# Hybrid SSD and attention step: four z tiles moved into the scan's code, the rest of the projection dealt out two query blocks later

## The chip, the cores and the metric

One core of one Trainium2 chip runs the whole program. The metric is device microseconds of one execution; lower is better. The kernel before takes 1961.51 us (median of 3 runs, 1960.96 to 1962.06).

## What is computed

One step of two trunk layers for 512 prompt tokens and 8 sample tokens (520 columns in all), width 1024. Layer 0 mixes a Mamba-2 scan and a sparse attention with one input and one output projection; layer 1 is a convolution module; a gated feed-forward network follows each. The change touches layer 0 alone:

```python
def ab_project(xn, pos, w_in):
    proj = xn @ w_in
    z, xbc, dt_raw, q, kvc, kvs, kvw, gates = jnp.split(proj, ...)
...
def mamba_branch(z, xbc, dt_raw, ...):
    xbc = jax.nn.silu(causal_dwconv(xh, conv_w, conv_b))
    xs, bm, cm = jnp.split(xbc, ...)
    ...
    y, h_T = ssd_scan(xs, dt, a, bm, cm, h0, SSM_CHUNK)
    y = y.astype(xs.dtype) + d_skip[:, None] * xs
    y = y.reshape(bsz, t, D_INNER) * jax.nn.silu(z)
    y = rms_norm(...)
...
def mixer_ab(xn, ...):
    y_ssm, new_hist, h_T = mamba_branch(...)
    y_nsa = nsa_fn(q, gates, kvc, kvs, kvw)
    out = jnp.concatenate([y_ssm, y_nsa], axis=-1) @ w_out
```

## The kernel before

Everything stands transposed, features on partitions and the 520 tokens in two halves of 256 and 264 columns. Float32 products are made of three products of split operands (`mm3`, L311 to L313: high by high, high by low, low by high), so one 128-row tile of a projection is 8 x 3 x 2 = 48 matmuls.

The mixer of layer 0 has these stages. The queries, keys and values are projected and the sample's cache is compressed (to 270 us). Then come 40 **xz tiles** (`xz_tile`, L992): ten for each of the scan's four groups g, of which t = 0 to 3 are x, 4 and 5 are B and C (these six run through a causal convolution on VectorE), and t = 6 to 9 are z. Each tile is silu'd through a scratch tile (`u_`, `uc`, `uth`) and spilled to DRAM. The first 10 (XZ0) are written ahead of the attention, the others inside it: 16 **query blocks** (4 head groups of 4 blocks; block b of a group attends to b + 1 key blocks, so the fourth is the largest), and after block `step` the code issues the tiles that the table XZF gives it (L1213):

```python
for n in range(*(XZ0 + int((40 - XZ0) * XZF[i]) for i in (step, step + 1))):
    xz_tile(n // 10, n % 10)
```

Next is the **scan** (`scan_group`, L1300): 4 groups of 4 row tiles t, which read the spilled x, z, B and C back. Beside the scan runs the output projection: `nsa_out` (L1286) loads the attention's result (8 `ynl` tiles), splits each into a high and a low part (`x0hn`, `x0ln`, `x1hn`, `x1ln`), and returns `part`, which makes one of 8 output tiles of 48 matmuls (`wo`). It is called once ahead of the first group, and `beside(t)` calls `part` as the table PARTS says. Groups 0 and 1 are then normalised (`gated`), split, and projected beside groups 2 and 3.

The order of the work on each engine is not that of the code: the program is built with a list scheduler that pulls an instruction forward where its operands, buffers and engine are free by its own timeline. It can carry a tile across the blocks and stages around it. The `zt` buffers (3, tag "zt") are shared by the z tiles of the scan and by `ynl`; the split input of the projection (`x0hm`, `x1hm` and their low parts) and that of the output projection (`x0hn` and so on) share one buffer each, so no `ynl` can be split before the last xz tile's products are done.

Of the kernel before, what the change touches and what calls it, by code (L numbers as in the profile page):

```python
# [11 lines left out]
F32 = mybir.dt.float32  # L12
# [13 lines left out]
T = S + NB  # L26
# [8 lines left out]
XZ0 = 10  # L35
# [24 lines left out]
SKEW = (3, 2)  # L60
SQN = 4
PARTS = (0, 0, 0, 3, 0, 0, 2, 2, 0, 0, 0, 3, 0, 0, 2, 2)
XZF = tuple(n / 16 for n in range(17))
VTB = 2
BES = (2, 1)
NST = 16
# [191 lines left out]
def step_kernel(ctx: ExitStack, tc: tile.TileContext, I, O):  # L258
# [423 lines left out]
    def mixer(begin):  # L682
# [25 lines left out]
        ux = ExitStack()  # L708
        up = ux.enter_context(tc.tile_pool(name="mu", bufs=1, side="right"))
        uth = up.tile([128, T], F32, name="uth")  # L710
        ax = ExitStack()
        ap = ax.enter_context(tc.tile_pool(name="ma", bufs=1))

# [4 lines left out]
        vnew = ap.tile([64, 128], F32, name="vnew")  # L718
        pnT = ap.tile([64, 128], F32, name="pnT")
        pti = ap.tile([1, 64], I32, name="pti")  # L720
        u_ = ap.tile([128, T], F32, name="u")
        uc = ap.tile([128, T], F32, name="uc")
        hp = ap.tile([128, 24, NB], F32, name="shp")
        stg = ap.tile([128, 24, 11], F32, name="sstg")
# [7 lines left out]
        for hf in range(2):  # L732
            x.append(tp.tile([128, KD, 266], F32, tag="big", bufs=BIG, name="x"))
            n = HALF[hf][1] - X0[hf]
# [227 lines left out]
        for op in ORDER.split():  # L962
            n = int(op[1:])
# [26 lines left out]
        turns = []  # L990
# [109 lines left out]
        def attention(hg, rows_of):  # L1100
# [3 lines left out]
            for b in range(4):  # L1104
# [105 lines left out]
                        sample(step)  # L1210
                for _ in range(HCN[step]):
                    next(rows_of, None)
                for n in range(*(XZ0 + int((40 - XZ0) * XZF[i]) for i in (step, step + 1))):  # L1213
                    xz_tile(n // 10, n % 10)

        def group_loads(g, q=nc.sync):
# [38 lines left out]
            pass  # L1255
        group, rows = group_loads(0, nc.gpsimd), row_loads(0, 0, nc.gpsimd)
        sample_end()
        nc.sync.dma_start(O["o_sc"], stg.rearrange("p a b -> p (a b)"))
        bp.close()
        ax.close()  # L1260
# [157 lines left out]

        sn4 = tp.tile([128, 16], F32, name="sn4")
        nc.vector.tensor_scalar_mul(sn4, VV("sn"), 0.25)  # L1420
        part = nsa_out()
        todo = iter(range(8))
        for kg in range(2):
            for g in (2 * kg, 2 * kg + 1):

                def beside(t):
                    for m in itertools.islice(todo, PARTS[4 * g + t]):
                        part(m)
                scan_group(g, beside)
            for g in (2 * kg, 2 * kg + 1):  # L1430
                gated(g)
            for m in todo:
                part(m)
            yx = {hf: new_x("s", hf) for hf in range(2)}
            for g in (2 * kg, 2 * kg + 1):
                parted(g, yx)
            if kg == 0:
                todo = iter(range(8))

                def part(m, yx=yx):  # L1440
                    w = wout(0, m)
                    for hf in range(2):
                        out_block(0, yx, m, hf, w, False)
# [252 lines left out]
```

## Time and profile before

| what | before |
|---|---|
| median of 3 runs | 1961.51 us |
| profiled execution, its own time | 1961.93 us |
| its span in the trace | 1959.4 us |
| TensorE (PE) busy | 93% of the span |
| VectorE (DVE) busy | 73% |
| ScalarE (ACT) busy | 50% |
| attention, blocks 0 to 15 | 272 to 667 us |
| last product of an xz tile | 609 us |
| scan, from its first product of states to the last group's | 672 to 836 us |

A matmul's duration in a row is its latency: the next one starts long before it ends. What a matmul costs the engine is read from the distance between two starts. The granted clock (PEclk) is a share of full speed: 1.00 is 2.4 GHz, 0.50 is 1.2 GHz, and a number between is a stretch with both.

### The profile page before, as it was taken

The page shows a single profiled execution, that of the slowest core. Times are in us where ns is not written, and L with a number is a line of the kernel's source. Part 1 is how long each engine was busy: PE and PEld are TensorE (multiplying, and loading weights), DVE is VectorE, ACT ScalarE, POOL GpSimd, SP SyncE. Part 2 cuts the span into 40 slices and gives each one's busy share as a digit, 9 for nine tenths or more (in the row PEclk, how much of TensorE's full clock was granted, in tenths as well). Part 3 has the DMA queues.
Part 4 walks back from the last instruction along what each step waited for, and adds up shares of the span by engine and source line. Part 5 has one row for each costly group of instructions (what it writes and reads, how often), then busy time and mean ns, then how long its engine had stood idle before and what let it go on. Part 6 is the DMA issues. An engine that isn't in the chain of part 4 may idle for free.

```text
span 1959.4 us, 37959 instructions
## 1 busy us (share of the span) xinstructions
PE 1822.2 (93%) x14411; PEld 1702.3 (87%) x14411; DVE 1424.0 (73%) x3404; ACT 971.4 (50%) x2091; POOL 184.1 (9%) x226
## 2 busy tenths in 40 slices
PE   6998899999998799998999999997998899999997
PEld 5997888988887588988999999987867889999997
DVE  5764768888887698968667766575776865666766
ACT  3223546676666577656555433354126755444433
POOL 0000021111000013130000211000100000000000
PEclk9999998999998799999999999998998999999999
DMA  8446254444421274543245433221443223333411
GB/s 289 120 139 191 77 195 130 144 145 123 132 90 55 87 244 138 162 137 106 86 139 170 132 105 109 87 80 52 103 138 104 87 86 113 122 122 120 149 62 49
DMA packets 125946, 240.89 MB, mean 123 GB/s; under 512 B 16499, under 2 KB 63236, under 8 KB 125444
## 3 DMA queue, kind: packets, MB, share of 16 engines
q1 hardware_dynamic: 120676, 221.45, 36.6%
q0 software_dynamic: 4000, 13.73, 2.3%
q10 hardware_dynamic: 1088, 3.29, 0.5%
q8 instruction: 113, 1.85, 0.4%
q14 instruction: 69, 0.57, 0.1%
HBM read 200.75 MB, written 30.88 MB: 118 GB/s over the span
## 4 chain that ended last, share of the span: by engine, by line
PE 41%; DVE 6%; ACT 3%; DMA 2%; SPq 2%; issue 2%; POOL 0%; DVEq 0%; ACTq 0%; POOLq 0%
PE up L311 8%; PE up L312 8%; PE up L313 8%; PE dn L311 4%; PE dn L312 4%; PE dn L313 4%; SPq L607 2%; PE pw L311 1%; PE pw L312 1%; PE pw L313 1%; PE dn L622 1%; DVE sq L328 1%; DVE facc L629 1%; DVE xf L384 1%; DVE h L386 1%
## 5 line engine op out<-in xcount | busy, mean ns | idle before, releaser
L311 PE MATMUL dn<-gh,wh_dn 128*128 128x256 f32 (+1 forms) x704 | 197.4, 285 | 3.3 <-ACT gh L462 2.6
L313 PE MATMUL dn<-gh,wl_dn 128*128 128x256 f32 (+1 forms) x704 | 198.6, 283 | 0.0
L312 PE MATMUL dn<-gl,wh_dn 128*128 128x256 f32 (+1 forms) x704 | 198.2, 283 | 0.0
L450 DVE SCALAR_TENSOR_TENSOR c<-up,vec,c 128x511 f32<-128x511 f32 (+2 forms) x216 | 139.0, 646 | 15.0 <-ACT c L447 14.6
L311 PEld LDWEIGHTS dn<-gh,wh_dn 128*128 128x128 f32 x704 | 131.5, 188 | 4.7 <-ACT gh L462 2.9
L312 PEld LDWEIGHTS dn<-gl,wh_dn 128*128 128x128 f32 x704 | 132.9, 189 | 0.2
L313 PEld LDWEIGHTS dn<-gh,wl_dn 128*128 128x128 f32 x704 | 132.5, 188 | 0.0
L463 POOL TENSOR_TENSOR gl<-gm,gh 128x520 fp32r<-128x520 f32 (+2 forms) x54 | 61.8, 1144 | 702.4 <-ACT gh L462 702.3
L445 DVE TENSOR_TENSOR up<-up,rsx 128x520 f32<-128x520 f32 (+2 forms) x108 | 65.0, 604 | 82.9 <-PE up L313 81.0
L477 DVE TENSOR_TENSOR facc<-dn,facc 128x256 f32<-128x256 f32 (+1 forms) x160 | 66.3, 424 | 66.6 <-PE dn L313 66.3
L292 ACT ACTIVATE wh_up<-raw_up 128x1024 fp32r<-128x1024 f32 x68 | 72.0, 1058 | 70.2 <-PE up L312 47.0
L311 PE MATMUL acc<-x0hm,wh_xz 128*128 128x256 f32 x320 | 96.8, 302 | 5.8 <-ACT u L999 3.4
L293 DVE TENSOR_TENSOR wl_up<-raw_up,wh_up 128x1024 fp32r<-128x1024 f32 x68 | 83.1, 1222 | 20.8 <-ACT wh_up L292 20.4
L313 PE MATMUL acc<-x0hm,wl_xz 128*128 128x256 f32 x320 | 95.0, 297 | 0.0
L312 PE MATMUL acc<-x0lm,wh_xz 128*128 128x256 f32 x320 | 94.7, 296 | 0.0
L447 ACT ACTIVATE c<-up,vec 128x520 f32<-128x520 f32 (+2 forms) x108 | 74.8, 695 | 36.3 <-DVE up L445 35.7
L312 PE MATMUL acc<-x1lm,wh_xz 128*128 128x264 f32 x320 | 92.7, 290 | 0.0
L311 PE MATMUL acc<-x1hm,wh_xz 128*128 128x264 f32 x320 | 92.6, 289 | 0.0
L313 PE MATMUL acc<-x1hm,wl_xz 128*128 128x264 f32 x320 | 92.2, 288 | 0.0
L292 ACT ACTIVATE wh_dn<-raw_dn 128x1024 fp32r<-128x1024 f32 (+1 forms) x48 | 47.4, 988 | 89.0 <-PE dn L312 63.6
L293 DVE TENSOR_TENSOR ptl<-pT,pth 128x512 fp32r<-128x512 f32 (+1 forms) x96 | 65.0, 684 | 25.4 <-ACT pth L292 25.1
L292 ACT ACTIVATE pth<-pT 128x512 fp32r<-128x512 f32 (+1 forms) x96 | 56.2, 595 | 51.5 <-PE pT L1184 49.5
(584 smaller groups left out, 6851.1 us busy)
## 6 DMA issues: line engine op xcount, KB each, us to landing
raw_up<-in_w_up SPq DMA_DIRECT2D x68, 512.0 KB, 3.7
raw_xz<-in_w_in SPq DMA_DIRECT2D x40, 512.0 KB, 4.8
raw_dn<-in_w_down SPq DMA_DIRECT2D x32, 512.0 KB, 3.6
raw_wo<-in_w_out SPq DMA_DIRECT2D x24, 512.0 KB, 4.4
raw_pw<-in_w_pw SPq DMA_DIRECT2D x24, 512.0 KB, 3.6
spill<-uth SPq DMA_DIRECT2D x40, 260.0 KB, 2.0
st<-in_st SPq DMA_DIRECT2D x40, 256.0 KB, 3.9
cc<-in_c_cmp SPq DMA_DIRECT2D x64, 128.0 KB, 2.6
```

The source lines that it names most:

```text
L292: nc.scalar.activation(hi, src, AF.Copy)
L293: (eng or nc.vector).tensor_sub(lo, src, hi.bitcast(F32))
L311: nc.tensor.matmul(ps, hi[:, wc], xh, start=first, stop=False)
L312: nc.tensor.matmul(ps, hi[:, wc], xl, start=False, stop=False)
L313: nc.tensor.matmul(ps, lo[:, wc], xh, start=False, stop=last)
L328: nc.vector.tensor_add(acc[:, :n], acc[:, :n], sq[:, :n])
L445: nc.vector.tensor_mul(u(a, e0), u(a, e0), rv[:, a:e0])
L447: nc.scalar.activation(c[:, rs], u(r0, r1), AF.Identity, bias=V("fb", l * 44 + mt), scale=W(2, mt))
L450: nc.vector.scalar_tensor_tensor(c[:, a:e], u(a - d, e - d), W(2 - d, mt), c[:, a:e], op0=ALU.mult, op1=ALU.add)
L463: nc.gpsimd.tensor_sub(gl[:, rs], gm[:, rs], gh[:, rs].bitcast(F32))
L477: nc.vector.tensor_add(f, ps, f)
L607: nc.sync.dma_start(x4[m][j * 32:j * 32 + 32, i, a:b], glu[m][i * 32:i * 32 + 32, 1 + j + a:1 + j + b])
```

## The change

Three things are edited. The table XZF is zero for the first two query blocks and deals out its tiles over the other 14, and it deals out 36 - 10 = 26 tiles instead of 30 (XZ1). The last four (group 3, t = 6 to 9, all z) are issued two at a time in `beside(0)` and `beside(1)` of group 0's scan, and `nsa_out` is called behind them, in `beside(1)`, instead of ahead of the scan. The scratch tile `u_` moves to a pool that lives through the scan, and small transposes that are left over (`turns`) are made behind the attention. The number of instructions of the projection, the attention and the scan is the same.

```diff
-XZF = tuple(n / 16 for n in range(17))
+XZF = tuple(max(n - 2, 0) / 14 for n in range(17))
+XZ1 = 36
...
         uth = up.tile([128, T], F32, name="uth")
+        u_ = up.tile([128, T], F32, name="u")
...
-        u_ = ap.tile([128, T], F32, name="u")
...
-                for n in range(*(XZ0 + int((40 - XZ0) * XZF[i]) for i in (step, step + 1))):
+                for n in range(*(XZ0 + int((XZ1 - XZ0) * XZF[i]) for i in (step, step + 1))):
                     xz_tile(n // 10, n % 10)
...
         sample_end()
+        for f in turns:
+            f()
+        turns.clear()
...
-        part = nsa_out()
+        part = None
         todo = iter(range(8))
+        late = iter(range(XZ1, 40))
         for kg in range(2):
             for g in (2 * kg, 2 * kg + 1):
 
                 def beside(t):
+                    nonlocal part
+
+                    for n in itertools.islice(late, 2):
+                        xz_tile(n // 10, n % 10)
+                    if g == 0 and t == 1:
+                        part = nsa_out()
                     for m in itertools.islice(todo, PARTS[4 * g + t]):
                         part(m)
```

What the scheduler makes of it shows in three places.

**TensorE, the end of block 13 and the beginning of block 14.** `sc` are the scores (128x32 the compressed branch, 128x384 block 14's own), `po` the products with the values, `acc<-...xz` the projection. Before, behind block 14's first scores:

```order
L1122 MATMUL sc<-KL_162,QS 128x32
L1197 MATMUL po<-pth,VB 128x512
L1121 MATMUL sc<-KH_160,QS 128x384
L1122 MATMUL sc<-KL_162,QS 128x384
L1198 MATMUL po<-ptl,VB 128x512
```

The same place in the changed kernel:

```order
L1123 MATMUL sc<-KL_163,QS 128x32
L314 MATMUL acc<-x0hm,wl_xz 128x256
L1198 MATMUL po<-pth,VB 128x512
L312 MATMUL acc<-x0hm,wh_xz 128x256
L313 MATMUL acc<-x0lm,wh_xz 128x256
L1122 MATMUL sc<-KH_161,QS 128x384
L1123 MATMUL sc<-KL_163,QS 128x384
L314 MATMUL acc<-x0hm,wl_xz 128x256
L312 MATMUL acc<-x0hm,wh_xz 128x256
L1199 MATMUL po<-ptl,VB 128x512
```

Products of xz tiles now stand between those of blocks 13 and 14, where there were none. Counted from the first scores of one block to those of the next, 48 products to a tile, the orders have (block 0 to the beginning of block 12, then block by block): before 28.5 tiles, then 3.2 in block 12, 0.3 in block 13, 0 in blocks 14 and 15; in the changed kernel 27.5, then 1.4 in block 12, 1.4 in block 13, 1.7 in block 14 and 0 in block 15. All 40 tiles, the four late ones too, stand ahead of block 15's scores.

**TensorE, the beginning of the scan.** `states`, `yd`, `yo` and `xT` are products of the scan, `wo` the output projection of the attention's result. Before:

```order
L1347 MATMUL states<-xde,BT 128x128 x4
L1370 MATMUL yd<-dc,xdt 64x128
L1375 MATMUL yo<-Cm,hst 128x128
L311 MATMUL acc<-x0hn,wh_wo 128x256
L1375 MATMUL yo<-Cm,hst 128x128
L311 MATMUL acc<-x1hn,wh_wo 128x264
L1370 MATMUL yd<-dc,xdt 64x128 x7
L1339 MATMUL xT<-cst_77,xs 128x128 x4
L312 MATMUL acc<-x0ln,wh_wo 128x256
```

In the changed kernel:

```order
L1351 MATMUL states<-xde,BT 128x128 x4
L1343 MATMUL xT<-cst_77,xs 128x128 x4
L1374 MATMUL yd<-dc,xdt 64x128
L1379 MATMUL yo<-Cm,hst 128x128 x2
L1374 MATMUL yd<-dc,xdt 64x128 x7
L1379 MATMUL yo<-Cm,hst 128x128
L1351 MATMUL states<-xde,BT 128x128 x4
L1343 MATMUL xT<-cst_77,xs 128x128 x4
L312 MATMUL acc<-x0hn,wh_wo 128x256
```

The `wo` products come later and the scan's own stand closer together: by the states of group 1's first row tile 144 `wo` products (3 tiles) are done before, and 38 (0.8 of a tile) in the changed kernel; by group 1's last row tile it is 5.5 and 5.25 tiles, by group 2's first 8.8 and 8.65.

**SyncE's DMA queue, the beginning of the scan.** Before:

```order
L1644 DMA d_yn_111<-ysS 256x1x8
L1290 DMA ynl<-d_yn_108 128x520 x2
L1290 DMA ynl<-d_yn_109 128x520
L1226 DMA xs<-spill_113 128x520
L1229 DMA cum<-d_rows 128x1056
L1226 DMA xs<-spill_114 128x520
```

In the changed kernel:

```order
L1655 DMA d_yn_111<-ysS 256x1x8
L1333 DMA zt<-spill_118 128x520
L1227 DMA xs<-spill_113 128x520
L1230 DMA cum<-d_rows 128x1056
L1333 DMA zt<-spill_119 128x520
L1294 DMA ynl<-d_yn_108 128x520
L1227 DMA xs<-spill_114 128x520
```

Three loads of the attention's result stood ahead of the second row tile's x (`spill_113`) and decay rows (`cum`); now one z tile does, and seven of the eight `ynl` loads come behind the loads of the row tiles t = 1 to 3.

## Rows read from the trace of the kernel before

**Rows 1.** The page: span; then busy time (share of the span) and instructions.

```profile
span 1959.4 us, 37959 instructions
PE 1822.2 (93%) x14411; PEld 1702.3 (87%) x14411; DVE 1424.0 (73%) x3404; ACT 971.4 (50%) x2091; POOL 184.1 (9%) x226
```

**Rows 2.** Windows by stage: blocks 4 to 11, 12, 13 and 14, 15; the scan.

```profile
core 0: us, PE busy (x) PEld busy (x) DVE busy (x) ACT busy (x) POOL busy (x), PEclk, DMA share, GB/s
372.00:471.00 99.00, 96.49 (x758) 87.81 (x757) 87.52 (x287) 65.79 (x164) 10.35 (x16) 1.00 0.47 140
471.00:571.00 100.00, 97.58 (x759) 89.07 (x757) 86.41 (x281) 65.39 (x163) 9.35 (x14) 0.98 0.43 131
571.00:609.00 38.00, 36.30 (x299) 33.24 (x299) 27.51 (x87) 21.24 (x56) 0.00 (x0) 1.00 0.26 75
609.00:630.00 21.00, 15.83 (x67) 10.56 (x65) 16.59 (x54) 13.29 (x39) 0.00 (x0) 0.76 0.16 51
630.00:667.00 37.00, 31.75 (x124) 20.74 (x124) 25.64 (x66) 19.47 (x43) 0.00 (x0) 0.77 0.03 8
667.00:700.00 33.00, 24.31 (x168) 19.98 (x170) 27.11 (x96) 24.11 (x66) 2.12 (x2) 0.90 0.75 245
700.00:760.00 60.00, 58.32 (x504) 54.98 (x500) 56.56 (x194) 45.34 (x112) 6.57 (x6) 1.00 0.66 213
760.00:780.00 20.00, 16.49 (x102) 14.28 (x103) 17.61 (x31) 11.99 (x32) 12.66 (x16) 0.91 0.32 90
```

**Rows 3.** Timeline of TensorE: two neighbouring products of an xz tile, and the last one.

```profile
600.17 0.28 PE L311 MATMUL acc<-x0hm,wh_xz 128*128 128x256 f32 x1
600.29 0.28 PE L312 MATMUL acc<-x0lm,wh_xz 128*128 128x256 f32 x1
...
608.78 0.28 PE L313 MATMUL acc<-x1hm,wl_xz 128*128 128x264 f32 x1
```

**Rows 4.** Timeline of TensorE: first scores of blocks 4 to 7, 9 to 15.

```profile
372.94 0.28 PE L1121 MATMUL sc<-KH,QS 128*128 128x32 f32 x1
405.86 0.18 PE L1121 MATMUL sc<-KH,QS 128*128 128x32 f32 x1
419.07 0.18 PE L1121 MATMUL sc<-KH,QS 128*128 128x32 f32 x1
441.49 0.18 PE L1121 MATMUL sc<-KH,QS 128*128 128x32 f32 x1
...
502.44 0.28 PE L1121 MATMUL sc<-KH,QS 128*128 128x32 f32 x1
517.86 0.18 PE L1121 MATMUL sc<-KH,QS 128*128 128x32 f32 x1
543.52 0.28 PE L1121 MATMUL sc<-KH,QS 128*128 128x32 f32 x1
570.61 0.18 PE L1121 MATMUL sc<-KH,QS 128*128 128x32 f32 x1
601.61 0.18 PE L1121 MATMUL sc<-KH,QS 128*128 128x32 f32 x1
611.92 0.28 PE L1121 MATMUL sc<-KH,QS 128*128 128x32 f32 x1 [1.51 <-ACT pt L1167]
629.99 0.28 PE L1121 MATMUL sc<-KH,QS 128*128 128x32 f32 x1 [0.55 <-ACT pt L1167]
```

**Rows 5.** Timeline of VectorE at the beginning of the scan.

```profile
669.98 0.16 DVE L1306 TENSOR_TENSOR bcs<-Bm,Cm 128x8 f32<-128x8 f32 x1
681.85 0.34 DVE L1389 TENSOR_TENSOR smp<-xs,cum 64x8 f32<-64x8 f32 x2 [2.10 <-DMA cum<-d_rows]
700.78 0.42 DVE L293 TENSOR_TENSOR x1ln<-ynl,x1hn 128x264 fp32r<-128x264 f32 x1
714.31 1.22 DVE L293 TENSOR_TENSOR wl_wo<-raw_wo,wh_wo 128x1024 fp32r<-128x1024 f32 x1
```

**Rows 6.** Timeline of TensorE: states of the scan's third group.

```profile
776.05 1.98 PE L1347 MATMUL states<-xde,BT 128*128 128x128 f32 x8 [0.86 <-DVE xde L1342]
```

## Prediction

> **What bounds the kernel now.** I read the page first: TensorE is busy 93% of the span, VectorE 73% [rows 1]. The average hides the stages, so the windows come next [rows 2]. The reader is to see three kinds of stretch in them. From 372 to 609 us, where xz tiles fill the attention, TensorE is busy 96 to 98% at full clock and VectorE 72 to 88%: TensorE sets the pace there, with VectorE not far behind. From 609 to 667 us, after the last xz product [rows 3], TensorE is busy 47.6 of 58 us at a mean granted clock of 0.76 to 0.77, so about 36 us of work at full clock were done in 58: some 21 us of TensorE are lost to gaps and to stretches at the lower level, 1.2 GHz. In the scan both engines are nearly full from 700 to 760 us (58.3 and 56.6 of 60), while in its first 33 us TensorE has gaps (24.3 busy, clock 0.90) and VectorE is busy 27.1.
>
> A row gives a matmul 0.28 us, but the next one starts 0.12 us later [rows 3]. A tile of 48 products thus costs TensorE 48 x 0.12 = 5.8 us where it is the bound. The 21 us lost are room for 3.7 tiles.
>
> **What the change does, by the order.** The words say that four z tiles go beside the scan. They don't: the scheduler pulls them forward, and all 40 tiles are issued before block 15. What the change really does is spread: one tile less before block 12, 1.8 less in block 12, 1.1 more in block 13, 1.7 more in block 14. And because `nsa_out` stands later in the code, the `wo` products that filled the beginning of the scan come later, with no xz tile in their place.
>
> **Term 1, blocks 0 to 11: one tile less.** In TensorE's stretch that is worth up to 5.8 us, and nothing if VectorE (87.5 of 99, 86.4 of 100, [rows 2]) holds those blocks. TensorE is the nearer bound (96.5 and 97.6), so I take -5; ends -5.8 and 0.
>
> **Term 2, block 12: 1.8 tiles less.** It lasts 31.0 us with 3.2 tiles, and block 4, of the same shape, 32.9 us with the 4.1 that its order holds [rows 4]; the difference of 1.9 us over 0.9 tile is only 2.1 us a tile, so -3.8 at the small end. At full price it is 1.8 x 5.8 = -10.4. The window of this very block has TensorE at 36.3 and VectorE at 27.5 of 38 us [rows 2], so it is nearest to the full price: -9.
>
> **Term 3, block 13: 1.1 tiles more.** It lasts 10.3 us with 0.3 tile; block 9, of the same shape, lasts 15.4 us with 1.35 tiles [rows 4], which is just what the change gives block 13 (1.4). So +5; ends +2 (most of it in TensorE's gaps) and +6.4 (1.1 x 5.8).
>
> **Term 4, block 14: 1.7 tiles more.** It lasts 18.1 us with none; block 6 lasts 22.4 with 1.8 and block 10 25.7 with 2.0 [rows 4]. Those two also carry a sample's gather and tiles with convolution taps on VectorE, while block 14 gets z tiles without taps. From block 6 it would be 22.4 - 0.1 x 5.8 - 18.1 = +3.7, from block 10 some +6; if the tiles only fill gaps, 0. I take +2.5.
>
> **Term 5, block 15.** No tile before or after; 37 us at clock 0.77 [rows 2, 4]. It can begin at the higher clock now, or meet its slow stretch at another place: 0, ends -2 and +2.
>
> Attention together: -5 - 9 + 5 + 2.5 = **-6.5 us**. The bounds don't fall on one side together; I use -13 to +1.
>
> **Term 6, the scan.** Before, the last `ynl` split ends VectorE's first 31 us (669.98 to 700.78, [rows 5]); from there the `wo` products run with all eight inputs. In the new order VectorE has as much work ahead of its last `ynl` split as it had before ahead of the instruction at 714.31 [rows 5]: 44 us, 13 us later. Until then TensorE can finish one `wo` tile, while before it has 2.5 done by that time (counted in the order): 1.5 x 5.8 = 8.7 us of products are late. Some 2 us of the scan's own products are early instead, because they no longer stand behind `wo`. So TensorE enters the common stretch 6.7 us behind. Three things give some back. The second row tile's decay row waits behind three `ynl` loads no more: VectorE's wait of 2.10 us [rows 5] goes for the most part. VectorE is ahead by the splits that it has not yet done. And around 760 to 780 us TensorE is busy only 16.5 of 20 us at clock 0.91 [rows 2], waiting for groups 0 and 1 to be normalised; in the new order more `wo` products stand behind that place and can cover the wait. The two orders meet at group 2's states (776.05, [rows 6]), where 8.8 and 8.65 tiles are done. I take **+1.5 us**; ends -3 (the waits gone, the hole covered) and +7 (nothing given back). In this the queue is included: on SyncE the second `ynl` load waits for VectorE's product with the first z row, and behind it stand loads of `cum`, `xs` and `st` for which ScalarE's decay rows and VectorE wait; its price lies between 0 and twice the 2.10 us.
>
> The other edits cost nothing. `u_` in another pool is the same memory for longer, and the left-over transposes are the same instructions, pulled to their old place. They have no cover to lose.
>
> **Sum.** -6.5 + 1.5 = -5.0. The profiled execution took 1961.93 us, its span 1959.4 with 2.5 us around it; the median of the runs is 0.42 lower. So 1961.5 - 5 = **1956.5 us**. About 0.2%, 3.9 us, is what a measurement tells from no change: faster is below 1957.6, slower above 1965.4.
>
> The Trainium skill, page Perfetto Trace Analysis, section Identifying the Most-Contended Engine, says that matmul busy time is no good measure of TensorE's headroom and that the busy share of weight loads is. By that share the filled stretch stands at 87 to 89%, not at 96 to 98; with terms 1 and 2 cut to 0.88 of their size the sum would be -3.3 and the time 1958.2. No run here shows yet which of the two measures holds.
>
> **Rivals.**
>
> *A wash (0.24).* VectorE, at 86 to 88% in blocks 4 to 11, may hold the blocks as much as TensorE; then a tile taken away gives back half: -3 and -6, against +5 and +3.7 where they are added, so about 0, and +1 with the scan: 1962.5. For it speaks the small slope from block 12 to block 4; against it that TensorE's window is fuller everywhere.
>
> *The hole at the scan's beginning decides: slower (0.17).* TensorE loses its filler at 667 us, the place to which the old hole (609 to 667) is carried. Without filler it ran at 0.76 to 0.77 there [rows 2]; if the 44 us to the last split run at 0.77 instead of 0.90, that is 44 x 0.13 = 5.7 us of TensorE's time on top of the 6.7, so the scan grows by 10 or more when nothing is given back. With an attention that gains only 4 it is +6: 1967.5. It decides if the way from the last block's end to group 2's states (106 us now, from 669.98 to 776.05, [rows 5, 6]) takes over 113 us. Against it: VectorE is the busier engine in the scan's first 33 us, so slow products may be hidden.
>
> The Trainium skill, page TensorE: Matmul & The Clock Gate, section HAM oscillation, speaks against the change in the same way: repeated lulls let the clock fall to half, and the next work starts slow. The trace before agrees with the direction (0.77 without filler against 1.00 with it).
>
> *All of it pays (0.12).* If TensorE alone bounds blocks 0 to 12 and the added tiles go into gaps, terms 1 to 4 are -5.8 - 10.4 + 2 + 0 = -14, and the scan stays as it is: 1947.5. The 21 us lost before 667 us allow it; block 9's 15.4 us speak against it.
>
> **How the numbers follow.** My forecast has 0.47; its own range, 1952 to 1961, lies for three quarters on the faster side of 1957.6 (0.36) and for the rest within 0.2% (0.11). The wash gives 0.19 to the same and 0.05 to slower, the hole 0.16 to slower and 0.01 to the same, the last rival 0.12 to faster. Faster 0.48, same 0.31, slower 0.21. The range for 8 in 10 takes in most of the hole's case and half of the last one's: 1948 to 1967.
>
> **What would show it.** Right: the last xz product near 610 us still, but block 15's first scores near 623 us instead of 630; TensorE's clock in blocks 13 and 14 near 1.00; the attention's end near 660 us. In the scan, `wo` products in force only some 44 us after its beginning, and 107 to 109 us from that to group 2's states. Wrong: block 12 longer than 25 us (term 2), block 14 longer than 22 us (term 4), or a scan that is 6 us longer (term 6).

## The result and the profile after

The changed kernel takes 1973.15 us (median, 1966.9 to 1978.08) beside 1961.51 for the kernel before on the same chip: ratio 1.0062, 95% interval 1.005 to 1.0075. It is slower by 11.6 us, three times what a measurement tells from no change, and outside the range of the prediction (1948 to 1967). The profiled execution took 1973.94 us.

The page of the changed kernel, span and busy times, beside [rows 1]:

```profile
span 1972.2 us, 37954 instructions
PE 1828.5 (93%) x14411; PEld 1707.6 (87%) x14411; DVE 1423.6 (72%) x3404; ACT 969.9 (49%) x2091; POOL 180.8 (9%) x226
```

The busy times of the other engines are what they were or less. TensorE is busy 6.3 us more and idle 6.5 us more in a span that is 12.8 us longer, at the same mean granted clock (0.965), so the totals don't say where the loss lies. The windows of the changed kernel over the stretches of [rows 2], same columns:

```profile
372.00:471.00 99.00, 96.69 (x733) 87.61 (x731) 84.75 (x279) 65.81 (x162) 9.02 (x16) 0.98 0.45 136
471.00:571.00 100.00, 96.51 (x744) 86.11 (x743) 85.44 (x280) 64.62 (x160) 7.96 (x13) 0.98 0.40 122
571.00:609.00 38.00, 33.18 (x245) 28.99 (x242) 30.18 (x99) 20.95 (x60) 0.50 (x1) 0.96 0.21 69
609.00:630.00 21.00, 21.00 (x157) 19.33 (x154) 14.37 (x41) 12.89 (x36) 0.00 (x0) 1.00 0.27 83
630.00:667.00 37.00, 30.95 (x125) 20.44 (x125) 27.66 (x71) 22.76 (x50) 0.00 (x0) 0.82 0.09 29
667.00:700.00 33.00, 22.42 (x151) 17.41 (x151) 26.52 (x97) 22.77 (x64) 2.00 (x2) 0.86 0.68 225
700.00:760.00 60.00, 55.98 (x443) 50.47 (x442) 52.45 (x179) 41.36 (x106) 6.12 (x5) 0.96 0.69 211
760.00:780.00 20.00, 19.56 (x156) 18.90 (x154) 15.75 (x33) 15.45 (x40) 9.74 (x12) 1.00 0.34 104
```

From 609 to 630 us TensorE is full at 1.00 now (15.83 of 21 at 0.76 before): that hole is filled, as planned. The stretches on both sides of it are less full. From 571 to 609 us, which now holds block 12 and 12.6 us of block 13, TensorE is busy 33.18 of 38 us where it was 36.30. In the first 93 us of the scan it is busy 78.40 us at 0.86 and 0.96 where it was 82.63 us at 0.90 and 1.00.

TensorE's timeline of the changed kernel, first scores of blocks 12 to 15 and the last xz product, beside [rows 3, 4]:

```profile
571.30 0.18 PE L1122 MATMUL sc<-KH,QS 128*128 128x32 f32 x1
596.45 0.26 PE L1122 MATMUL sc<-KH,QS 128*128 128x32 f32 x1
611.34 0.18 PE L1122 MATMUL sc<-KH,QS 128*128 128x32 f32 x1
628.96 0.37 PE L314 MATMUL acc<-x1hm,wl_xz 128*128 128x264 f32 x1
632.93 0.32 PE L1122 MATMUL sc<-KH,QS 128*128 128x32 f32 x1
```

Blocks 12, 13 and 14 last 25.2, 14.9 and 21.6 us (31.0, 10.3 and 18.1 before), and attention ends at 668.25 (last `otmp` of ScalarE; 667.37 before). Nothing was gained there.

The scan of the changed kernel, beside [rows 5, 6]. First VectorE's timeline: its first row, the last `ynl` split, and group 2's mask (`cbm`, VectorE's first row of that group). Then TensorE's: the first states, the first `wo` product, and group 2's states.

```profile
670.86 0.16 DVE L1310 TENSOR_TENSOR bcs<-Bm,Cm 128x8 f32<-128x8 f32 x1
...
716.65 0.42 DVE L294 TENSOR_TENSOR x1ln<-ynl,x1hn 128x264 fp32r<-128x264 f32 x1
777.66 0.68 DVE L1324 TENSOR_TENSOR cbm<-cb,cst 128x512 f32<-128x512 f32 x1
```

```profile
672.96 0.57 PE L1351 MATMUL states<-xde,BT 128*128 128x128 f32 x3 [1.48 <-ACT dc L1368]
685.20 0.39 PE L312 MATMUL acc<-x0hn,wh_wo 128*128 128x256 f32 x1 [1.17 <-ACT x0hn L293]
...
781.40 0.79 PE L1351 MATMUL states<-xde,BT 128*128 128x128 f32 x5 [1.75 <-DVE xde L1346]
```

Of the kernel before, the first `wo` product and group 2's mask:

```profile
676.14 0.58 PE L311 MATMUL acc<-x0hn,wh_wo 128*128 128x256 f32 x1 [0.20 <-ACT x0hn L292]
...
771.34 0.68 DVE L1320 TENSOR_TENSOR cbm<-cb,cst 128x512 f32<-128x512 f32 x1
```

The last `ynl` split comes 45.8 us after the first row (30.8 before), the first `wo` product 9 us later, group 2's states 5.3 us later (781.40 against 776.05).

That is less than half of the loss. Followed further, the two traces part at two places more. The lag, row against row: 4.5 us at the first `up` product of layer 0's feed-forward (905.62 against 901.16), 8.5 at its first product with a `wh_up` tile (971.39 against 962.93), the same 8.5 at the conformer's first `pw` product (1312.66 against 1304.19; the conformer is layer 1's convolution module, `pw` its pointwise projections), 13.5 at its last (1485.00 against 1471.45), 12.7 at the last row. So some 4 us are lost in the feed-forward's first 62 us and 5 in the `pw` products: stages that the diff doesn't touch. What TensorE waits for there, before and after:

```profile
930.59 0.55 PE L311 MATMUL up<-x0ha,wh_us 128*128 128x256 f32 x1 [3.27 <-DVE c L450]
...
1339.73 0.39 PE L311 MATMUL pw<-x0hb,wh_pw 128*128 128x256 f32 x1 [1.03 <-ACT glu L585]
```

```profile
937.51 0.55 PE L312 MATMUL up<-x0ha,wh_us 128*128 128x256 f32 x1 [5.57 <-DVE c L451]
952.03 0.36 PE L312 MATMUL up<-x1ha,wh_us 128*128 128x266 f32 x1 [1.77 <-DVE c L451]
...
1350.73 0.58 PE L312 MATMUL pw<-x0hb,wh_pw 128*128 128x256 f32 x1 [3.50 <-ACT glu L586]
```

In the feed-forward TensorE waits until VectorE's convolution (`c`) gives a buffer of `up` back. The order of the program says why it waits longer. VectorE, at the feed-forward's beginning, before:

```
1521 L386 TENSOR_TENSOR h<-h,xf 128x264 x2
1522 L384 SCALAR_TENSOR_TENSOR xf<-facc,vec,rs_11560 128x264 x2
1523 L366 SCALAR_TENSOR_TENSOR x1la<-h,vec,x1ha 128x266
1524 L386 TENSOR_TENSOR h<-h,xf 128x264
1525 L445 TENSOR_TENSOR up<-up,rsx 128x256
...
1532 L450 SCALAR_TENSOR_TENSOR c_11780<-up,vec,c_11780 128x255
```

and in the changed kernel:

```
1521 L387 TENSOR_TENSOR h<-h,xf 128x264 x2
1522 L385 SCALAR_TENSOR_TENSOR xf<-facc,vec,rs_11560 128x264 x2
1523 L367 SCALAR_TENSOR_TENSOR x1la<-h,vec,x1ha 128x266
1524 L387 TENSOR_TENSOR h<-h,xf 128x264 x2
1525 L367 SCALAR_TENSOR_TENSOR x1la<-h,vec,x1ha 128x266
...
1528 L446 TENSOR_TENSOR up<-up,rsx 128x256
...
1534 L451 SCALAR_TENSOR_TENSOR c_11780<-up,vec,c_11780 128x255
```

The scaling of the `up` buffer and its convolution stand behind more of the post-norm's rows. The diff doesn't touch these stages; the scheduler dealt them out anew behind another mixer.

### The profile page after: what moved, and what is told of

The parts are those of the page before. It is cut to its first block, busy times and chain, and to the rows that moved or that the text cites. A ratio compares the mean times of both kernels' runs of the same rounds, so it can differ in the third digit from the quotient of the medians.

```text
span 1972.2 us, 37954 instructions
## 1 busy us (share of the span) xinstructions
PE 1828.5 (93%) x14411; PEld 1707.6 (87%) x14411; DVE 1423.6 (72%) x3404; ACT 969.9 (49%) x2091; POOL 180.8 (9%) x226
## 4 chain that ended last, share of the span: by engine, by line
PE 41%; DVE 6%; ACT 3%; DMA 2%; SPq 2%; issue 2%; POOL 0%; DVEq 0%; ACTq 0%; POOLq 0%
PE up L312 8%; PE up L313 8%; PE up L314 8%; PE dn L312 5%; PE dn L313 5%; PE dn L314 5%; SPq L608 2%; PE pw L312 1%; PE dn L623 1%; DVE xf L385 1%; PE pw L313 1%; DVE sq L329 1%; PE pw L314 1%; DMA raw_us<-in_w_up 1%; DVE facc L630 1%
## 5 line engine op out<-in xcount | busy, mean ns | idle before, releaser
L464 POOL TENSOR_TENSOR gl<-gm,gh 128x520 fp32r<-128x520 f32 (+2 forms) x54 | 61.8, 1145 | 704.6 <-ACT gh L463 704.5
L478 DVE TENSOR_TENSOR facc<-dn,facc 128x256 f32<-128x256 f32 (+1 forms) x160 | 66.2, 423 | 66.1 <-PE dn L314 65.6
L293 ACT ACTIVATE wh_dn<-raw_dn 128x1024 fp32r<-128x1024 f32 (+1 forms) x48 | 47.4, 988 | 88.6 <-PE dn L313 63.4
```

Of the source, the lines that this page charges most:

```text
L293: nc.scalar.activation(hi, src, AF.Copy)
L464: nc.gpsimd.tensor_sub(gl[:, rs], gm[:, rs], gh[:, rs].bitcast(F32))
L478: nc.vector.tensor_add(f, ps, f)
```

## The experiments

Three theories: A, the spread of the tiles is a wash; B, the late `wo` projection costs the scan's 5 us; C, the rest is the order of the instructions behind the mixer. Rival of A (A'): a tile is worth the 5.8 us of the prediction. Rival of C (C'): the rest follows from a scan that ends late, or is one execution's clock.

All runs in one table. From the profile of each: the end of attention (last `otmp`); the scan, from its first states to group 2's mask; FF, the feed-forward's beginning, from the first `up` product to the first with a `wh_up` tile; pw, from the first to the last `pw` product. FF order and pw order: in how many rows the order of VectorE around FF's beginning, and of TensorE in pw, differs from the kernel before / from the change. A moved row seems to count at both its places: in the traces 51 rows of TensorE have moved where the table has 100, and 32 where it has 62. The expectations measure FF to a later `dn` product instead (the 20th by their count, the 34th `dn` row of FF in the traces): 86.7 before, 90.7 in the change, and in runs 11, 13 and 14 88.6, 93.2 and 91.1. The stages are those of one profiled execution; in runs 3 and 4 it took 1978.64 and 1982.10 us, more than 7 us over the median.

| run | median us, ratio to before [95%] | attention end | scan | FF | FF order | pw | pw order |
|---|---|---|---|---|---|---|---|
| before | 1961.51 | 667.4 | 99.2 | 61.8 | 0/27 | 167.3 | 0/100 |
| change | 1973.15, 1.0062 | 668.2 | 104.7 | 65.8 | 27/0 | 172.3 | 100/0 |
| 1 spread alone | 1953.43, 0.9961 [0.9946, 0.9976] | 665.2 | 96.8 | 63.6 | 25/32 | 167.0 | 2/100 |
| 2 wo early | 1971.51, 1.0055 [1.0039, 1.0072] | 668.2 | 99.3 | 66.5 | 27/0 | 168.7 | 6/100 |
| 3 wo late | 1971.04, 1.0050 [1.0032, 1.0068] | 668.7 | 104.3 | 69.1 | 27/0 | 169.5 | 20/50 |
| 4 late, old spread | 1974.82, 1.0073 [1.0052, 1.0094] | 669.7 | 104.9 | 68.3 | 27/0 | 173.9 | 100/2 |
| 5 fences, before | 1998.37, 1.0183 | 665.9 | 96.0 | 49.7 | as 6 | 155.9 | as 6 |
| 6 fences, change | 2012.17, 1.0254 | 668.3 | 107.4 | 49.4 | as 5 | 155.9 | as 5 |
| 7 tiles held | 1976.60, 1.0079 [1.0055, 1.0103] | 656.0 | 116.3 | 66.8 | 19/20 | 172.4 | 20/50 |
| 8 held, wo early | 1969.78, 1.0050 [1.0031, 1.0069] | 650.4 | 124.7 | 62.6 | 6/28 | 167.9 | 62/88 |
| 9 control | 1960.11, 0.9995 [0.9984, 1.0006] | 664.4 | 98.2 | 62.2 | 0/27 | 168.8 | 0/100 |
| 10 other order | 1960.63, 0.9999 [0.9987, 1.0010] | 666.4 | 100.2 | 61.2 | 8/30 | 168.0 | 62/88 |
| 11 own order | 1966.75, 1.0023 [1.0010, 1.0037] | 666.5 | 98.6 | 63.7 | 54/33 | 168.3 | 44/62 |
| 12 in the change | 1973.68, 1.0063 [1.0045, 1.0081] | 667.2 | 103.2 | 69.2 | 39/12 | 169.3 | 6/100 |
| 13 change again | 1974.80, 1.0055 [1.0037, 1.0072] | 671.4 | 103.3 | 68.3 | 27/0 | 172.5 | 100/0 |
| 14 as 2, again | 1970.96, 1.0046 [1.0032, 1.0060] | 669.0 | 101.0 | 66.2 | 27/0 | 169.6 | 6/100 |
| 15 as 4, again | 1976.90, 1.0083 [1.0069, 1.0097] | 665.1 | 104.3 | 65.7 | 27/0 | 174.6 | 100/2 |
| 16 as 1, again | 1954.86, 0.9956 [0.9943, 0.9969] | 666.5 | 97.4 | 63.8 | 25/32 | 166.7 | 2/100 |

**Runs 1 and 16: the new spread alone.**

```diff
-XZF = tuple(n / 16 for n in range(17))
+XZF = tuple(max(n - 2, 0) / 14 for n in range(17))
```

> Edit: the kernel before with the new spread alone (no tile in the first two query blocks, all 40 dealt out by the end); the wo projection of the scan keeps its place, and the instructions of the feed-forward and of the conformer's beginning stand as before. Theory A (a projection tile fills idle TensorE time in a query block, so moving it is a wash): last attention output within 2 us of before's 667.4, total 1961.5 +/- 2. Rival A' (the price of the prediction, 5.8 us for each tile moved, with block 15 free): attention ends 4 to 8 us earlier, total 1954 to 1957.

> Edit: before with the new spread alone (as run 1) with the same multiplication, orders as in run 1. If its gain is the order of its scan (which run 5, with the old spread, shared): attention ends within 2 us of before's 664 to 667, scan 98 to 99 us against 103 to 105, total 1952 to 1957. If the gain was the spread's: attention ends 4 or more us earlier.

Attention ends at 665.2 and 666.5, within the 664.4 to 668.7 of the five executions that have before's order there (before and runs 3 and 9 to 11): the spread gives attention nothing that these executions could show, and for attention A holds. For the total it doesn't: A had 1961.5 for run 1, and the kernel is faster than before (0.9961 and 0.9956). Its scan is 2 us shorter, and run 5, which has the old spread, shares that (96.0); from the last `pw` product to the end it takes 481.7 and 481.8 us where before takes 484.7. FF is dealt out anew, against the expectation (25/32), and takes 2 us more. None of this is what the edit was about. Which rows of its order bring the gain was not tried.

**Runs 2 and 14: the wo projection early again.** Run 14, as runs 13, 15 and 16, has besides one multiplication by 1.0 of eight columns that leaves every engine's order as it was.

```diff
-        part = None
+        for n in range(XZ1, 40):
+            xz_tile(n // 10, n % 10)
+        part = nsa_out()
...
-                    for n in itertools.islice(late, 2):
-                        xz_tile(n // 10, n % 10)
-                    if g == 0 and t == 1:
-                        part = nsa_out()
```

> Edit: the change with one thing undone: the four held-back tiles and the preparation of the wo projection (nsa_out) are issued ahead of the scan's loop, as before's is; attention's order and the order from the feed-forward on are the change's. Theory B (the late wo projection costs the 5.3 us of the scan): first states of group 2 at 776 to 777.5, not 781.4. Theory C (the rest of the loss, 3.2 us at the feed-forward's beginning and 4.8 us at the conformer's, comes from the order of the instructions there, which differs from before's): total 1961.5 + 0 + 8 = 1967 to 1971. Rival C' (the rest is a consequence of the late scan, or of the clock that an engine kept waiting gets): with the scan in time again nothing is left, total 1961 to 1964.

> Edit: the change with the wo early (as run 2) with the same multiplication, orders as in run 2. Scan 104 +/- 1. If the order sets the stages behind the mixer: feed-forward 91 to 94, pointwise products as in run 2 (168 to 170), total 1966 to 1969 and 3 to 5 us under the change on the same chip. If the pointwise products come out at 172 to 174, the execution sets them and not the order, and the total is 1970 to 1972.

B holds: the scan is back at 99.3 and 101.0 us. FF keeps the change's order and takes 66.5 and 66.2 us, with the scan in time: that is C against its rival. About the conformer the expectation of run 2 rests on an order that I had misread: the `pw` products stand as before but for six rows, not as in the change, and they take 168.7 and 169.6 us, not 172. Read so, that speaks for C as well. The total of run 2, 1971.51, lies 0.5 us over C's range. On one chip run 14 is 3.8 us under run 13, but its total lies above the expected 1966 to 1969; its profiled execution (1973.35) had attention 1.6 us and the scan 1.8 us over before's, and why the median is high is not shown.

**Run 3: the wo projection late, nothing else.**

```diff
-        part = nsa_out()
+        part = None
...
+                    nonlocal part
+                    if g == 0 and t == 1:
+                        part = nsa_out()
```

> Edit: the kernel before with one thing of the change alone: nsa_out is issued beside the second scan block of group 0. Attention is before's. The order at the feed-forward's beginning is the change's, that at the conformer's beginning nearly before's (the pointwise products keep before's order). Theory B: group 2's states 4 to 6 us later than 776.05 (780 to 782). Theory C: another 2 to 4 us at the feed-forward's beginning, 0 to 2 at the conformer's; total 1961.5 + 5 + 3 + 1 = 1968 to 1972. Rival C': the same loss as the whole change, 1973 to 1975, or the scan's 5 alone, 1966 to 1967. If the late wo projection does not cost, group 2's states stay at 776.

The scan takes 104.3 us: B on its own makes nearly the whole of the scan's loss. FF, in the change's order, takes 69.1; pw, nearer to before's order, 169.5. The total, 1971.04, is in C's range.

**Runs 4 and 15: the change with the old spread.**

```diff
-XZF = tuple(max(n - 2, 0) / 14 for n in range(17))
+XZF = tuple(n / 16 for n in range(17))
```

> Edit: the change with the old spread of the tiles (36 of 40 dealt out from the first block on); all else as in the change, the order of feed-forward and conformer too. Theory A with B and C: attention within 2 us of the change's 668.3, group 2's states about 113 us after the scan's first, total 1973 +/- 2. Rival A': attention is 4 to 8 us longer than the change's, total 1977 to 1981.

> Edit: the change with the old spread (as run 4) with the same multiplication, orders as in run 4, behind the mixer the same as in run 14. Scan 108 to 109, total within 2 us of run 13. Pointwise products: 172 to 174 if a late scan brings the loss there, 168 to 170 if it was the execution's.

Attention ends at 669.7 and 665.1, the change's at 668.2 and (run 13) 671.4: A holds, its rival falls. Behind the mixer this kernel has the change's order (100/2 rows at pw; run 14 has not, against what is said of it in the expectation), and its `pw` products take 173.9 and 174.6 us. So the conformer's 5 us are no accident of one execution: they come back wherever its order does. All four executions of that order (the change, runs 4, 13 and 15) stand behind a late scan, and none behind a scan in time was made. A late scan alone doesn't bring the 5 us: runs 3 and 12 have one, and their `pw` products take 169.5 and 169.3 us.

**Runs 5 and 6: fences.** One barrier over all engines ahead of the feed-forward and one ahead of the conformer, in either kernel.

```diff
+    tc.strict_bb_all_engine_barrier()
     x2, rs2, after = boundary("b", 0, 3, 1, 0)
...
+    tc.strict_bb_all_engine_barrier()
     conformer(x2, rs2, after, chp)
```

> Edit: the kernel before with two barriers over all engines, one ahead of the feed-forward of layer 0 and one ahead of the conformer, so that what the scheduler does downstream does not depend on the mixer. Only its difference to the next run counts. The barriers themselves cost what work crossed them: 0 to 30 us against 1961.5.

> Edit: the changed kernel with the same two barriers. From the first barrier on its instructions stand as in the run before this one but for one pair of rows. Theory C (downstream the change loses by the order of the instructions): against the fenced kernel before only the mixer's difference is left, 4 to 7 us (the scan's 5.3). Rival C' (it loses downstream because the scan comes late, or by a clock that follows the mixer): the whole 11 to 14 us stay.

The fences cost 36.9 us in the kernel before, over the 0 to 30 expected. By the totals the rival seemed to win: 13.8 us stay. By the stages it is the other way. The fences changed the mixers' orders too, and the whole difference is there: the last `wo` product starts at 899.1 and 913.6, 14.5 us apart; then the same order takes the same time, FF 49.7 and 49.4, pw 155.9 and 155.9, and the ends of the traces are 14.0 us apart. A scan that ends 14 us late costs nothing further when the order behind it is the same. A barrier also keeps work of the mixer from reaching across it, so this alone doesn't tell what a late scan does where no barrier stands; run 8 does for FF, and runs 3 and 12 for pw.

**Runs 7 and 8: the four tiles really beside the scan.**

```diff
                     for n in itertools.islice(late, 2):
-                        xz_tile(n // 10, n % 10)
+                        with tc.issue_after(behind_t[0].ins):
+                            xz_tile(n // 10, n % 10)
```

`behind_t[0]` is the last `yo` product of the scan's row tile. Run 8 issues `nsa_out` ahead of the loop besides.

> Edit: the change with each of the four held-back tiles chained behind the last yo product of its scan block, so that they do lie beside the scan (in the change the scheduler pulls them into the last query blocks). Attention from block 13 on loses four tiles: at the 3.2 us that a tile of block 12 was worth, attention ends near 655, at the forecast's 5.8 us near 645. The scan takes four tiles of 5.8 us of TensorE against some 8 us that TensorE stood idle or at the low clock between 673 and 723: group 2's states 128 to 133 us after attention's end (113 in the change). Together a wash: total 1971 to 1979; if the scan hides the tiles (its VectorE sets the pace until 730), 1958 to 1964.

> Edit: as the run before, with the preparation of the wo projection issued ahead of the scan's loop again (nsa_out where the kernel before has it). Theory B: the wo products still come behind the tiles on TensorE, but their operands are ready, so the scan is 0 to 5 us shorter than in the run before; the order downstream is another again, worth -4 to +4: total 1964 to 1976. If the late wo projection was what cost in the scan even with the tiles beside it, 1966 to 1969.

Windows of run 7 (end of attention, beginning of the scan, the rest to group 2):

```profile
640.00:660.00 20.00, 15.63 (x72) 11.40 (x72) 11.74 (x28) 7.97 (x15) 0.00 (x0) 0.77 0.06 14
660.00:700.00 40.00, 36.20 (x295) 33.95 (x296) 32.75 (x136) 26.57 (x69) 2.02 (x2) 0.91 0.81 264
700.00:780.00 80.00, 76.86 (x619) 70.79 (x617) 65.00 (x168) 58.90 (x151) 17.95 (x16) 1.00 0.59 189
```

In run 7 attention ends 12.2 us earlier (656.04 for 668.25); the scan grows by 11.6, and group 2's mask stands at 777.07, where the change has 777.66. A wash, although TensorE is busy 36.20 of the 40 us in which the change has its hole: VectorE has its own 32.75 us there. In run 8 attention ends 17.9 us earlier than in the change and the scan grows by 20.0: the mask stands at 779.85.

The first scores of block 12 in runs 7 and 8:

```profile
573.15 0.18 PE L1122 MATMUL sc<-KH,QS 128*128 128x32 f32 x1
567.55 0.18 PE L1122 MATMUL sc<-KH,QS 128*128 128x32 f32 x1
```

Up to there the order of TensorE, VectorE and ScalarE is the change's in both (but for one pair of VectorE's rows at 205 us), so these 5.6 us are the executions'. From there to attention's end both take 82.9 us, 14.1 less than the change: 3.5 us a tile. B expected run 8's scan no longer than run 7's, and it is 8.4 us longer: with the tiles ahead of them on TensorE, the early operands of `wo` bring nothing (first `wo` product at 700.87, in run 7 at 699.08). But FF, in an order near before's, takes 62.6 us after a late scan.

Runs 3 and 7 stand equally far from both `pw` orders (20/50), and the stage takes 169.5 and 172.4 us. In run 7, as in runs 4 and 15 and not in run 3, TensorE waits for VectorE's squares (`sq`) at a sum of the norm (`ns`):

```profile
1353.67 1.25 PE L333 MATMUL ns<-sq,ones 128*128 128x264 f32 x2 [4.45 <-DVE sq L329]
```

How many rows stand otherwise says little; which ones do decides.

**Runs 9, 10 and 11: before, with a multiplication by 1.0.** It is put behind an output tile of the mixer's last projection, to give the scheduler another order and leave the work as it is.

```diff
                 out_block(1, yx, m, hf, ws[m], False)
+                if (hf, m) == (1, 0):
+                    nc.vector.tensor_scalar_mul(facc[hf][:, m, :8], facc[hf][:, m, :8], 1.0)
```

Run 10 has `(1, 5)`; run 11 `(0, 5)`, and twice 256 columns.

> Control. Edit: the kernel before with one multiplication by 1.0 of eight columns of the accumulator, behind output tile 0 of the second half of the mixer's last projection. All five engines keep before's order. All theories: 1961.5 +/- 2, no difference to before.

> Edit: the same multiplication behind output tile 5 in place of 0. Up to the mixer's end the order is before's; the scheduler then deals the feed-forward's beginning out nearly as before and the conformer's beginning otherwise (near that of the run with the held tiles and the early wo). Theory C (order downstream is worth microseconds): the same as before to the mixer's end, then 0 to 1 us at the feed-forward, 1 to 4 at the conformer, total 1962 to 1966. Rival C' (no loss without a late scan): 1961.5 +/- 1.5.

> Edit: the kernel before with two multiplications by 1.0 of 256 columns behind output tile 5 of the first half (some 0.4 us each on VectorE). The mixer's order is before's but for its last 15 us; the feed-forward's beginning is dealt out as in the change but for six rows of VectorE, the conformer's beginning nearer the change's than before's. Theory C: scan in time, then from the first up product to the 20th down product 90 to 94 us (86.6 before) and 168 to 173 us of pointwise products (167.3 before), total 1966 to 1971. Rival C': no late scan, no loss: 1961 to 1963.

The control is equal to before. Run 10 is too: the `pw` products differ in 62 rows and cost 0.7 us, so C's 1 to 4 us there was wrong, and the total is where C' had it; not every other order is a worse one. In run 11 the order that I had named is not the one it has: FF has an order of its own (54/33 rows). It takes 63.7 us, and the last 15 us of the mixer, reordered too, some 2.7 more (the last `wo` product starts 4.0 us behind the first `up` product, 6.7 before). The kernel, whose scan is in time, is 5.7 us slower than before for two multiplications estimated at 0.8 us. Its total lies in C's range and over the 1961 to 1963 of C'; to the later `dn` product its FF takes 88.6 us, below C's 90 to 94.

**Runs 12 and 13: the change, with a multiplication.** Eight columns, run 12 behind `(1, 2)`, run 13 behind `(1, 0)`.

> Edit: the changed kernel with the multiplication of eight columns behind output tile 2 of the second half. Mixer and feed-forward's beginning keep the change's order; the conformer's beginning goes back most of the way to before's (13 rows of VectorE differ, not 40). Theory C: the change's 113 us of scan and 90 to 91 us at the feed-forward stay, the conformer's 5 us mostly go: 1968 to 1971. Rival C': 1973 +/- 1.5.

> Edit: the changed kernel with one multiplication by 1.0 of eight columns (output tile 0, second half), all orders as in the change. If its loss is a matter of order: scan 108 +/- 1 us, first up product to 20th down product 90 to 94, pointwise products 171 to 174, total 1972 to 1975. If the conformer's 5 us were that one execution's: pointwise products 167 to 170.

Run 12 has before's `pw` order but for six rows, and its `pw` products take 169.3 us, against 172.3 and 172.5 in the change and in run 13. At FF 12 rows differ from the change; it takes 69.2 us. From the last `pw` product to the end it takes 487.7 us where the change takes 483.9, and the total, 1973.68, stays where C' had it: C's forecast of pw held, that of FF (94.2 us to the later `dn` product, not 90 to 91) and of the total not, and what lengthens the end was not tried. Run 13, the change's order a second time, gives the stages back: 103.3, 68.3, 172.5.

What sets FF apart is read from one window of each, from the first `up` product to the first with `wh_up`: before, the change, run 13.

```profile
901.16:962.93 61.77, 51.67 (x365) 49.02 (x363) 50.05 (x113) 40.35 (x82) 7.34 (x9) 0.89 0.19 59
```

```profile
905.62:971.39 65.77, 51.09 (x365) 48.35 (x363) 50.10 (x114) 41.90 (x83) 7.59 (x9) 0.92 0.20 58
```

```profile
906.22:974.48 68.26, 54.24 (x365) 50.60 (x363) 50.98 (x115) 42.02 (x83) 7.42 (x9) 0.85 0.19 57
```

Idle time of TensorE: 10.1, 14.7 and 14.0 us. Time given away at the lower clock, length times (1 - clock): 6.8, 5.3 and 10.2. What is left is 44.9, 45.8 and 44.0: the work. The change's order costs 4 us of idle time in both executions; how much clock goes with it differs from one to the next by 5 us. In all seven executions with that order TensorE is idle for 13.6 to 15.1 us of FF, in the four with before's order or near it for 10.1 to 11.5.

The same for the scan, from its first states to group 2's mask, and for pw; before, then the change:

```profile
672.09:771.34 99.25, 89.83 (x721) 81.94 (x722) 88.72 (x287) 75.64 (x195) 16.93 (x19) 0.97 0.71 227
1304.19:1471.45 167.26, 151.81 (x1232) 125.40 (x1232) 123.86 (x219) 48.80 (x86) 15.31 (x26) 0.96 0.36 96
```

```profile
672.96:777.66 104.70, 92.19 (x712) 82.62 (x713) 87.71 (x290) 75.61 (x199) 15.51 (x17) 0.93 0.67 210
1312.66:1485.00 172.34, 153.86 (x1232) 126.92 (x1232) 124.49 (x219) 48.44 (x86) 15.40 (x26) 0.94 0.34 93
```

TensorE is idle 3.1 us more in the scan and 3.0 more in pw. The lower clock takes some 3 us in the scan before and some 7 in the change, and some 7 and 10 in pw. So in these two executions each of the two losses is about half waiting and half clock.

## Why the prediction was wrong

**Terms 1 to 5, attention: -6.5 forecast, +0.9 measured.** Block 12 begins at 571.30 (570.61 before): term 1 was +0.7, not -5. Its small end was nearest; seven executions of one order reach block 12 between 567.55 and 573.39. Term 2: block 12 is 5.8 us shorter, not 9; 1.8 tiles at 3.2 us each. Term 3: +4.6 (+5 forecast). Term 4: +3.5 (+2.5). Term 5: from block 15's first scores to the end 35.3 us, 37.4 before: -2.1 (0), but the control, in before's order, has 35.6. The step that failed is the price of a tile taken away, as length of the block: "So a tile costs TensorE 48 x 0.12 = 5.8 us where it is the bound", chosen against a slope of 2.1 us a tile that [rows 4] offered. Runs 7 and 8, which take four tiles out of attention altogether, give 3.5 us a tile. The wash that stood as a rival is what attention did, and runs 1, 4, 15 and 16 show no effect of the spread beyond what one order's executions differ by.

The windows of block 12, before and in the change, and the change's longest wait of TensorE in it, which block 12 before has not (in total, times, longest):

```profile
570.61:601.61 31.00, 29.30 (x239) 27.29 (x238) 21.91 (x60) 16.96 (x43) 0.00 (x0) 1.00 0.29 84
571.30:596.45 25.15, 20.33 (x135) 17.36 (x134) 19.87 (x63) 13.09 (x38) 0.50 (x1) 0.93 0.19 63
PE po L1199 <- DVE ptl L294: 3.4, 3, 1.5
```

TensorE is busy 9.0 us less for the 1.8 tiles, near the -9 of the forecast, but the block is only 5.8 us shorter: TensorE then waits for VectorE's split of the probabilities (`ptl`), idle 4.8 us in place of 1.7, at a clock of 0.93 in place of 1.00.

A busy share of 96% in [rows 2] was taken for a bound; with rows of 0.28 us that start 0.12 apart [rows 3] it holds latencies that overlap, while VectorE stands at 72 to 88% beside it and is what TensorE meets next. The Trainium skill, page Perfetto Trace Analysis, section Identifying the Most-Contended Engine, says to judge TensorE's headroom by its weight loads instead. The trace agrees in direction, not in size: by the 0.88 that the weight loads show a tile would be worth 5.1 us, and 3.2 to 3.5 were measured.

**Term 6, the scan: +1.5 forecast, +4.5 measured** to group 2's states (+5.3 with attention's 0.9), and +5.5 to its mask; runs 3, 4, 12, 13 and 15 lie between +4.0 and +5.7 to the mask. The mechanism was the one named: the last split 46 us into the scan (44 forecast), the `wo` products late by it. What failed is the sum of what is "given back": of 6.7 us it gave back 2, not 5. The way from the scan's beginning to group 2's states is 110.5 us, short of the 113 at which the rival of the hole was to decide, so by its own sign that rival doesn't decide. Its mechanism has a part: to the mask the lower clock takes 3 to 4 us more than before (0.93 for 0.97), where it feared 5.7, and idle time 3.1 us more. The Trainium skill, page TensorE: Matmul & The Clock Gate, section HAM oscillation, was cited for it: the trace agrees in direction.

**The step that was not there: everything behind group 2's states.** "The two orders meet at group 2's states", said term 6, and the sum ended there. The orders of the mixer meet; those of the feed-forward and of the conformer do not. They cost 4.0 and 5.1 us, more than all terms together. The terms alone, as measured, are +5.4 in place of -5.0: that turns the sign and gives 1966.9, the upper end of the range; the two stages bring the rest. Shown: the stages keep their length with the order, not with the scan. FF takes 61.2 to 62.6 us in the four executions with before's order or within eight rows of it, one of them after a late scan (run 8), and 65.7 to 69.1 in the seven with the change's, two of them after a scan in time (runs 2 and 14); fenced to the same order it is 49.7 and 49.4. The `pw` products take 166.7 to 168.8 us within two rows of before's order and 172.3 to 174.6 within two rows of the change's. The new wait for `c` at an `up<-x1ha` product (1.77 us at 952.03) stands in FF, with 1.8 to 2.2 us, in the traces of the change and of runs 2 to 4, 7 and 11 to 15, and in none of before and runs 1, 5, 6, 8 to 10 and 16. Only argued: that it is the later `up` scaling on VectorE, of all the rows moved, which makes TensorE wait in FF; moving that row alone was not tried.

The sum, from the profile: +0.9 attention, +4.5 scan, -0.9 to the first `up` product, +4.0 FF, 0 to the conformer, +5.1 `pw`, -0.8 to the end: +12.7 at the trace's last row, 12.8 of span.

Of the prediction's signs, the clock came (1.00 from 609 to 630 us) and so did `wo` in force only 46 us into the scan; block 15's first scores (632.93, not 623), attention's end (668, not 660) and block 12 (25.2 us, over 25) spoke against it. The last xz product, at 628.96 and not near 610, stands where term 4 puts it, in block 14; that sign didn't fit its own term. That the new spread alone (1953.4 and 1954.9 us) comes near the forecast's 1956.5 is luck, since its attention gains nothing.

## What to carry to other kernels

Where a scheduler orders the program, a change ends where the two orders are equal again, not where the edited code ends: compare them to the last row, and give each stage that is dealt out anew an uncertainty of its own, here 4 to 5 us. To judge a change of less than that, set barriers (which reorder what stands ahead of them too, as runs 5 and 6 show) or keep the order downstream, and read it by stages; a total can be made of the scheduler's luck, as run 1 shows from the good side.

A tile that is moved between two stretches is worth what the block gains when it goes, not its matmuls times their spacing, where another engine stands close behind in the same window: here 3.2 to 3.5 us, between the 2.1 us that blocks of one shape had offered and the 5.8 us of the spacing.

## What was not expected

A multiplication of eight columns leaves every order as it was (run 9), or, in another place, alters 62 rows of TensorE's order some 400 us further on, at no cost (run 10). A pair of 256 columns costs 5.7 us (run 11).

Executions of one order differ by some 4 us in where attention ends (664.4 to 668.7 in before's, 667.2 to 671.4 in the change's), while the `pw` stage of one order comes back within 1.6 us. And FF in one order is 65.8 or 68.3 us long by the clock, with no more idle time or work: granted 0.92 and 0.85, a mean between the levels of 1.2 and 2.4 GHz, with TensorE idle for 14.7 and 14.0 us of it.
